# One decoder layer on one core: reloading an overwritten piece of X during the last double pair, and the low parts of two of seven pieces split on GpSimd

## The chip, the cores and the metric

The kernel runs on one core of one Trainium2 chip. The metric is the device time of one execution in microseconds (us), as a median over runs. Engines are named as in the profile: PE is TensorE (matmul), DVE is VectorE, ACT is ScalarE, POOL is GpSimd, SP is SyncE, which here issues most DMA transfers.

## The reference, cut to what matters

One step of a hybrid decoder layer in fp32, for a prompt of 1024 tokens and 8 sample tokens, model width 1024, feed-forward width 2816:

```python
x = layer_norm(ALPHA*x + 0.5*swiglu_1(x))     # first FFN
z = x @ w_in + b_in                           # projection: q k v o i f | B C h | two gates
y_a = (head_norm(mLSTM(q,k,v,i,f)) * sigmoid(o)) @ w_a
y_b = (B * conv3(C*h)) @ w_b
x = layer_norm(ALPHA*x + (sigmoid(g_a)*y_a + sigmoid(g_b)*y_b) @ w_mix)
x = layer_norm(ALPHA*x + 0.5*swiglu_2(x))     # second FFN
x = layer_norm(ALPHA*x + sigmoid(x @ w_pg) * (p @ w_pp))
```

Also returned are the mLSTM and conv states of both groups.

## The kernel before, in words

The 1032 token columns are kept in two halves of 516, and each half is worked on in blocks of 256 and 260 columns. A fp32 matrix product is made of three matmuls on numbers split into a high and a low part of type fp32r: high by high, high by low, low by high (L590, L591, L592, or L231 to L233 in other places). A split is two instructions: ACT casts the number to the high part (L274 for X, L185 for data loaded from DRAM, L416 for weights), and DVE subtracts this from the number, which gives the low part (L275, L186, L417).

Large products are not made of eight block products but of seven (Strassen-Winograd). X, hidden activations and weights therefore exist in seven pieces, which are sums and differences of blocks. The function `pair` makes such a product for one pair of weight columns. `pair2` makes a double pair, two of them at once, and applies the seven-product form once more to one inner product. For that inner product `quarters` derives smaller pieces of X, and one of these, t4, is written over a piece of X itself (`XS[1]`, in code b12). The pairs after the last double pair read that piece of X again. So it has to be reloaded from DRAM and split again, two tiles of it (kp = 0, 1): a load by SP to a tile `tmp`, the cast L274, the subtract L275. In the two FFNs this is the inner function `redo`, called at the first single pair behind the last double pair (p = 10, loop over hidden pairs p from 1; double pairs are p = 3 to 9). In the projection the same lines stand behind the loop that ends with `conv_val(3)`, and the memory-state update of the sample group follows.

Finished hidden activations go to DRAM in seven pieces (`hsum`). The output layer of an FFN takes them back in groups of hidden pairs: 3, 3 and 2 in the first FFN, 3, 3 and 3 in the second. For a group, `split_load` loads each piece (j = 0 to 6 of each pair, 128x516) and splits it (L185 on ACT, L186 on DVE). Then `segment` runs for n = 0 to 3: it makes weight pieces (sums on DVE at L425 and L428 and on POOL at L426 and L433, splits at L416 and L417) and the seven products in order j. `add` (L898, DVE) adds each finished product from PSUM onto the residual tile in SBUF, which frees the PSUM tile for a later product. PSUM tiles come from three pools, called mm, aux and pn.

```python
if j == 3:
    add(1, s, ps, OP.subtract)
elif j == 5:
    add(1, s, ps)
    add(1, s + 2, ps)
```

The list `beside` holds functions by step number; a pair calls those of its step beside its own products. `at(k, f)` puts a function there. A scheduler with priorities sets the final order of each engine's instructions; each engine then runs its own queue in that order, and waits at an instruction until what it reads is there. So an instruction that waits holds all that stands behind it in its queue.

Of the kernel before, what the change touches and what calls it, by code (L numbers as in the profile page):

```python
# [12 lines left out]
OP = mybir.AluOpType  # L13
# [3 lines left out]
NT = 1032  # L17
# [12 lines left out]
HW = 516  # L30
BN = (256, 260)
BM = 260
BLK4 = [(i // 2 * HW + i % 2 * BN[0], BN[i % 2]) for i in range(4)]
# [3 lines left out]
def F_(ap):  # L37
    return ap.bitcast(F32)
# [25 lines left out]
def layer_kernel(ctx: ExitStack, tc: tile.TileContext, I, O):  # L64
    nc = tc.nc
    V, S, G, T, DQ = nc.vector, nc.scalar, nc.gpsimd, nc.tensor, nc.sync
# [28 lines left out]
    def tmp(n=BM):  # L95
        return tmpp.tile([128, BM], F32, name="tmp", tag="tmp")[:, :n]
# [76 lines left out]
                   gen(dst[i], R) if dst else None) for i, r in enumerate(rows)]  # L173
        return [[(hi[:, j, :], lo[:, j, :]) for hi, lo in t] for j in range(4)]

    def split_load(t, src, after=nullcontext):

        hi, lo = t
        DQ.dma_start(F_(lo), src)
        with after():  # L180
            return split_here(t)

    def split_here(t):
        hi, lo = t
        S.copy(hi, F_(lo))  # L185
        V.tensor_tensor(lo, F_(lo), F_(hi), op=OP.subtract)  # L186
        return hi, lo

    ahead = {"src": {}, "live": {}, "to": {}}
# [52 lines left out]
    def bs(t, b, blk=BLK):  # L242
        c0, n = blk[b]
        return t[:, c0:c0 + n]
# [21 lines left out]
    def xparts(X7, j, kp):  # L266
        t = X7[j][kp // 2]
        return t[:, 2 * (kp % 2)], t[:, 2 * (kp % 2) + 1]
# [4 lines left out]
    def hilo(dst, src):  # L273
        order_["hi"] = S.copy(dst[0], src).ins  # L274
        order_["lo"] = V.tensor_tensor(dst[1], src, F_(dst[0]), op=OP.subtract).ins  # L275
# [26 lines left out]


    QS = ["w4", "w5", "e0"]

    def quarters(XS):

# [40 lines left out]
    def wcomb2(ra, rb):  # L348

        def k4(t):  # L350
            return t[:, 0:512].rearrange("p (k n) -> p k n", n=128)

        def put(src):
            s = slot()
            return split((k4(s), k4(s[:, 512:1024])), src)

        def fresh():
            return rawp.tile([128, 512], F32, name="raw", tag="raw")

        def blocks(r):  # L360
            return [u[:, :, i:i + 128] for u in r for i in (0, 128)]

        def sums(r):
            a11, a21, a12, a22 = blocks(r)
            s1, s2, s3 = (k4(fresh()) for _ in range(3))
            V.tensor_tensor(s1, a21, a22, op=OP.add)
            G.tensor_tensor(s3, a11, a21, op=OP.subtract)
            V.tensor_tensor(s2, s1, a11, op=OP.subtract)
            return s1, s2, s3

        def rest(r, w, s1, s2, s3):
            w[2] = put(s2)
            w[3] = put(blocks(r)[3])
            w[4] = put(s1)
            G.tensor_tensor(s2, blocks(r)[2], s2, op=OP.subtract)
            w[5] = put(s3)
            w[6] = put(s2)
            return w

        def quarter():  # L380
            half = []

            def put2(src):
                if not half:
                    s = slot()
                    half.extend([s[:, i:i + 512] for i in (0, 512)])
                t = half.pop(0)
                return split(tuple(t[:, i:i + 256].rearrange("p (k n) -> p k n", n=128) for i in (0, 256)), src)

            a11, a12, a21, a22 = (u[1][:, k:k + 2, 0:128] for u in (ra, rb) for k in (0, 2))  # L390
            s1, s2, s3, s4 = (t.rearrange("p (k n) -> p k n", n=128) for f in (fresh(), fresh())
                              for t in f.rearrange("p (a m) -> a p m", a=2))
            q = {1: put2(a12), 0: put2(a11)}
            V.tensor_tensor(s1, a21, a22, op=OP.add)
            V.tensor_tensor(s2, s1, a11, op=OP.subtract)
            G.tensor_tensor(s3, a11, a21, op=OP.subtract)
            q[4], q[2] = put2(s1), put2(s2)
            G.tensor_tensor(s4, a12, s2, op=OP.subtract)
            q[3], q[5], q[6] = put2(a22), put2(s3), put2(s4)
            return q  # L400

        t = sums(ra)
        wa = rest(ra, {0: put(blocks(ra)[0])}, *t)
        wb = {0: put(blocks(rb)[0]), 1: quarter()}
        return wa, rest(rb, wb, *sums(rb))
# [188 lines left out]
    beside = []  # L594
# [149 lines left out]
    TWO = range(3, 10)  # L744

    def ffn(wi, wo, l, XS, enter, xlate, raws, sgs, RTs, res, groups, plains, tail, extra=None, aside=None, split=None):
        hsum = tc.dram_tile([7, NHID // 2, 128, HW], F32, name=f"hsum{l}")
# [36 lines left out]
        def wi_raw(p, k):  # L784
            i = 2 * p + k
            return wraw(wi, k * FF + p * 256, raws[2 * (i % 2):2 * (i % 2) + 2])
# [45 lines left out]
                            V.scalar_tensor_tensor(d, d, 0.5, ps, op0=OP.mult, op1=OP.mult)  # L832
                        DQ.dma_start(bs(hscr[i], c, BLK4), d)

        def redo(XS):
            for kp in range(2):
                t = tmp()
                DQ.dma_start(t, bs(res[4 + kp], 1, BLK4))
                hilo(xparts(XS[1], 1, kp), t)

        enter(plain, wearly)
        sreg()
        wr = wi_raw(1, 0)
# [3 lines left out]
        for p in range(1, NHID // 2):  # L847
            if p > 1:
                sg = [gen(sgs[2 * ((p + 1) % 2) + i]) for i in range(2)]
            if p == TWO[0] - 1:  # L850
                use_ring([i for i in ring["slots"] if i not in QS])
                late = quarters(XS)
                XQ = next(late)
                at = (3, 8, 19, 24)
                beside.extend([partial(next, late)] if i in at else [] for i in range(28))
            if p == TWO[0]:
                ahead_all(aside, 7 * 24 + 28)
            if p in TWO:
                def place(i, c):
                    return bs(sg[i], c, BLK4)  # L860

                def gate(i, c, t):
                    S.activation(t, t, AF.Silu)

                def up(i, c, t):
                    d = bs(sg[i], c, BLK4)
                    V.scalar_tensor_tensor(d, d, 0.5, t, op0=OP.mult, op1=OP.mult)

                pair2(wcomb2(wi_raw(p, 0), wi_raw(p, 1)), XS, XQ, (place, lambda i, c: None), (gate, up))
            else:  # L870
                if p == TWO[-1] + 1:
                    set_ring(QS + from_ring())
                    redo(XS)
                for k in range(2):
                    hidden(k, w0 if p == 1 and k == 0 else wcomb(wi_raw(p, k)), sg, p == 1 and k == 0)
            spill(p, sg)
# [38 lines left out]
        i = 0  # L915
        for ps_, slots in groups:
            parts = {}
            for j in range(7):
                for k, p in enumerate(ps_):
                    t = gen(slots[j * len(ps_) + k], R)  # L920
                    parts[j, k] = split_load((t[:, 0:HW], t[:, HW:NT]), hsum[j, p])
            for n in range(4):
                segment(ps_, parts, n, i)
                i += 1
                order_["add", n] = order_["add"]
# [107 lines left out]
    XP = x7()  # L1033
# [301 lines left out]
    def conv_first(w, then):  # L1335
        pre_ = sg_pair()

        def out_c(i, c, fn):
            fn(bs(pre_[i], c, BLK4))

        pair(w, XP, (0, 1), out_c, True)
        for i in range(2):
            S.activation(pre_[i], pre_[i], AF.Identity, bias=bcol(CC0, i))
        then()

        def product_in(d, c0):
            def out(i, c, fn):
                t = tmp(BN[c % 2])
                fn(t)
                times(d, c0, 0)(i, c, t)  # L1350

            pair(in_pair(c0), XP, (0, 1), out)

        product_in(pre_, CH0)
        y = sg_pair()
        for i in range(2):
            conv_y(i, pre_[i], y[i])
        product_in(y, CB0)
        for i in range(2):
            DQ.dma_start(yscr[i], y[i])  # L1360

    def conv(jj):
# [4 lines left out]
        for i in range(2):  # L1367
            at(1 + 4 * i, partial(conv_y, 2 * jj + i, pre_[i], y[i]))
        return y

    def at(k, f):
        beside.extend([] for _ in range(k + 1 - len(beside)))
        beside[k].append(f)

    def conv_val(jj, y):
        d = []
        at(7, lambda: d.extend(sg_pair()))
        pair2(wcomb2(in_raw(CB0 + jj * 256), in_raw(V0 + jj * 256)), XP, XQ, (own, whole(d)),
              (times(y, CB0, jj), done), (None, lambda i: bcol(V0, 2 * jj + i)))
        for i in range(2):  # L1380
            DQ.dma_start(yscr[2 * jj + i], y[i])
        val_end(jj, d)
# [193 lines left out]
    for h in range(1, 4):  # L1576
        keys(h)
        if h < 3:
            decays(4 * h - 4)
        y = conv(h)  # L1580
        if h < 3:
            decays(4 * h - 2)
        else:
            at(6, dec_pre)
            at(14, dec_dot)
        conv_val(h, y)
    set_ring(QS + from_ring())
    for kp in range(2):
        t = tmp()
        DQ.dma_start(t, bs(x2scr[4 + kp], 1, BLK4))  # L1590
        hilo(xparts(XP[1], 1, kp), t)

    if count["sg"] % 2:
        psgs = psgs[2:] + psgs[:2]
# [529 lines left out]
    for t, nm in ((gB, "ln_g"), (bB, "ln_b")):  # L2124
        src = I[nm][0, 3]
# [9 lines left out]
    t = gen(21, R)  # L2135
# [52 lines left out]
```

## Time and profile before

| | |
|---|---|
| runs | 2645.91, 2649.43, 2652.66 us; median 2649.43 |
| the profiled execution | 2654.4 us, its span 2652.6 us |
| mean granted PE clock | 0.998 |
| busy | PE 2614.9 us (99%), DVE 2021.6 (76%), ACT 1273.0 (48%), POOL 724.8 (27%) |

A line of a list of waits reads "engine, what it was about to do <- engine, what it waited for: us in total, times, longest". A line of a timeline reads "start, duration, engine, line, operation, written tile <- read tiles, shapes", and in brackets the idle time ahead of it with what ended it; equal neighbours are drawn together (x2). A line of windows gives the stretch, its length, then busy time and count of PE, weight load, DVE, ACT and POOL, then the granted PE clock, the busy share of the DMA engines and GB/s. A line of a source line or tile gives durations in ns as min/median/max.

### The profile page before, as it was taken

The numbers are of one execution on the slowest core, as the hardware profiler recorded it, in microseconds if no ns is written. First come the engines' busy times: TensorE is split into PE (matmuls) and PEld (weight loads), VectorE is DVE, ScalarE is ACT, GpSimd is POOL, SyncE is SP. The second block draws the span as 40 slices with busy tenths as digits, with TensorE's granted clock in tenths as the row PEclk, the third lists the DMA queues.
The fourth block names the chain that finished last, engine by engine and source line by source line (L and its number), as shares of the span: only waits on it lengthen the run. The fifth ranks groups of instructions, "written<-read, shape, count | busy, mean of one in ns | idle before, by whom it ended". The sixth has DMA issues, their size and how long they took to land.

```text
span 2652.6 us, 56341 instructions
## 1 busy us (share of the span) xinstructions
PE 2614.9 (99%) x21630; PEld 2578.3 (97%) x21630; DVE 2021.6 (76%) x4356; ACT 1273.0 (48%) x2863; POOL 724.8 (27%) x724
## 2 busy tenths in 40 slices
PE   9999999999999999999999999999999999999998
PEld 9999999999999999999999999999999999999998
DVE  6877787988988777685555677748878778888787
ACT  5444446533554544445566555415445454633241
POOL 2432331112432112121110344423343233111354
PEclk9999999999999999999999999999999999999999
DMA  6244456632143343426667776832435445644421
GB/s 210 93 144 167 149 176 232 205 128 69 48 150 101 100 136 89 128 69 196 193 190 236 231 240 216 294 113 101 130 101 184 164 159 195 240 136 135 175 74 57
DMA packets 327190, 408.38 MB, mean 154 GB/s; under 512 B 30233, under 2 KB 248809, under 8 KB 326921
## 3 DMA queue, kind: packets, MB, share of 16 engines
q1 hardware_dynamic: 304600, 383.54, 44.4%
q10 hardware_dynamic: 22320, 21.26, 2.8%
q8 instruction: 169, 2.77, 0.4%
q14 instruction: 101, 0.82, 0.1%
HBM read 273.11 MB, written 131.63 MB: 153 GB/s over the span
## 4 chain that ended last, share of the span: by engine, by line
PE 87%; DVE 7%; DMA 3%; ACT 2%; issue 1%; POOL 0%; SPq 0%; DVEq 0%; ACTq 0%; POOLq 0%
PE mm L590 14%; PE mm L591 14%; PE mm L592 14%; PE mm L231 6%; PE mm L233 6%; PE mm L232 6%; PE aux L590 5%; PE aux L592 5%; PE aux L591 5%; PE pn L231 2%; PE pn L233 2%; PE pn L232 1%; PE pn L590 1%; PE pn L592 1%; PE pn L591 1%
## 5 line engine op out<-in xcount | busy, mean ns | idle before, releaser
L590 PE MATMUL mm<-a,w 128*128 128x256 f32 (+1 forms) x2289 | 646.8, 283 | 3.4 <-DVE a L898 1.7
L591 PE MATMUL mm<-a,w 128*128 128x256 f32 (+1 forms) x2289 | 644.1, 282 | 0.6 <-DVE a L275 0.5
L592 PE MATMUL mm<-a,w 128*128 128x256 f32 (+1 forms) x2289 | 643.0, 282 | 0.0
L590 PEld LDWEIGHTS mm<-a,w 128*128 128x128 f32 x2289 | 430.7, 188 | 9.3 <-issue 3.8
L591 PEld LDWEIGHTS mm<-a,w 128*128 128x128 f32 x2289 | 430.9, 188 | 1.0 <-DVE a L275 1.0
L592 PEld LDWEIGHTS mm<-a,w 128*128 128x128 f32 x2289 | 430.6, 188 | 0.5 <-issue 0.4
L590 PE MATMUL aux<-a,w 128*128 128x256 f32 (+1 forms) x852 | 241.7, 284 | 5.1 <-ACT a L274 5.0
L591 PE MATMUL aux<-a,w 128*128 128x256 f32 (+1 forms) x852 | 240.2, 283 | 0.0
L592 PE MATMUL aux<-a,w 128*128 128x256 f32 (+1 forms) x852 | 239.1, 283 | 0.0
L433 POOL TENSOR_TENSOR raw<-a,raw 128x512 f32<-128x512 f32 (+2 forms) x52 | 63.8, 1227 | 563.4 <-DVE w L417 203.6
L231 PE MATMUL mm<-a,w 128*128 128x256 f32 (+4 forms) x727 | 208.0, 288 | 2.0 <-ACT w L1683 1.8
L232 PE MATMUL mm<-a,w 128*128 128x256 f32 (+4 forms) x727 | 207.1, 286 | 0.0
L590 PE MATMUL mm<-a,e 128*128 128x256 f32 (+1 forms) x694 | 196.7, 283 | 2.6 <-DVE a L898 1.5
L591 PE MATMUL mm<-a,e 128*128 128x256 f32 (+1 forms) x694 | 195.4, 282 | 0.0
L592 PE MATMUL mm<-a,e 128*128 128x256 f32 (+1 forms) x694 | 195.3, 281 | 0.0
L233 PE MATMUL mm<-a,w 128*128 128x256 f32 (+4 forms) x681 | 192.7, 286 | 0.0
L590 PEld LDWEIGHTS aux<-a,w 128*128 128x128 f32 x852 | 161.3, 189 | 7.6 <-ACT a L274 5.4
L591 PEld LDWEIGHTS aux<-a,w 128*128 128x128 f32 x852 | 161.4, 190 | 0.0
L592 PEld LDWEIGHTS aux<-a,w 128*128 128x128 f32 x852 | 160.7, 190 | 0.4 <-issue 0.4
L590 PE MATMUL mm<-a,cd 128*128 128x260 f32 (+1 forms) x520 | 147.4, 284 | 1.4 <-ACT sreg L623 0.6
L591 PE MATMUL mm<-a,cd 128*128 128x260 f32 (+1 forms) x520 | 146.8, 282 | 0.0
L344 ACT CAST w<-raw 128x512 fp32r<-128x512 f32 (+1 forms) x179 | 96.5, 549 | 104.7 <-PE aux L592 40.1
(629 smaller groups left out, 8274.0 us busy)
## 6 DMA issues: line engine op xcount, KB each, us to landing
a<-in_ffn_wi_dram SPq DMA_DIRECT2D x80, 512.0 KB
a<-in_w_in_dram SPq DMA_DIRECT2D x68, 512.0 KB
a<-hsum SPq DMA_DIRECT2D x119, 258.0 KB
wscr<-w SPq DMA_DIRECT2D x35, 512.0 KB
hsum<-a SPq DMA_DIRECT2D x68, 258.0 KB
a<-in_ffn_wo_dram SPq DMA_DIRECT2D x40, 384.0 KB
w<-wscr SPq DMA_DIRECT2D x25, 512.0 KB
a<-in_state_C_dram ACTq DMA_DIRECT2D x32, 256.0 KB
```

Source lines behind the costliest of these rows:

```text
L231: T.matmul(ps, wh, xh, start=(i == 0), stop=False)
L232: T.matmul(ps, wh, xl, start=False, stop=False)
L233: last = T.matmul(ps, wl, xh, start=False, stop=(i == n - 1))
L344: S.copy(dst[0], src)
L433: G.tensor_tensor(s4, a12, s2, op=OP.subtract)
L590: T.matmul(ps, wh, xh, start=start and kp == 0, stop=False, skip_group_check=True)
L591: T.matmul(ps, wh, xl, start=False, stop=False, skip_group_check=True)
L592: T.matmul(ps, wl, xh, start=False, stop=stop and kp == len(xs) - 1, skip_group_check=True)
```

## The change: earlier reloads, and 34 subtracts on POOL

There are three edits. First, `redo` no longer runs behind the last double pair: it puts the two loads at steps 16 and 17 and the two splits at steps 18 and 20 of that double pair's `beside` list. This holds for both FFNs and for the projection. Second, for pieces j = 5 and 6 (products six and seven) of the output layers, the subtract L186 runs on POOL. These are 34 instructions: 6, 6 and 4 in the first FFN's groups, 6, 6 and 6 in the second's. Third, in `conv_first` the second `conv_y` runs beside step 1 of the following product.

```diff
-    def split_load(t, src, after=nullcontext):
+    def split_load(t, src, after=nullcontext, eng=None):
         hi, lo = t
         DQ.dma_start(F_(lo), src)
         with after():
-            return split_here(t)
+            return split_here(t, eng)
 
-    def split_here(t):
+    def split_here(t, eng=None):
         hi, lo = t
         S.copy(hi, F_(lo))
-        V.tensor_tensor(lo, F_(lo), F_(hi), op=OP.subtract)
+        (eng or V).tensor_tensor(lo, F_(lo), F_(hi), op=OP.subtract)
...
+    def redo(XS, src):
+        t = {}
+        def load(kp):
+            t[kp] = tmp()
+            DQ.dma_start(t[kp], bs(src[4 + kp], 1, BLK4))
+        def split_(kp):
+            hilo(xparts(XS[1], 1, kp), t.pop(kp))
+        for kp in range(2):
+            at(16 + kp, partial(load, kp))
+            at(18 + 2 * kp, partial(split_, kp))
...
-        def redo(XS):
-            for kp in range(2):
-                t = tmp()
-                DQ.dma_start(t, bs(res[4 + kp], 1, BLK4))
-                hilo(xparts(XS[1], 1, kp), t)
...
+                if p == TWO[-1]:
+                    redo(XS, res)
                 pair2(wcomb2(wi_raw(p, 0), wi_raw(p, 1)), XS, XQ, (place, lambda i, c: None), (gate, up))
             else:
                 if p == TWO[-1] + 1:
                     set_ring(QS + from_ring())
-                    redo(XS)
...
-                    parts[j, k] = split_load((t[:, 0:HW], t[:, HW:NT]), hsum[j, p])
+                    parts[j, k] = split_load((t[:, 0:HW], t[:, HW:NT]), hsum[j, p], eng=G if j > 4 else V)
...
-        for i in range(2):
-            conv_y(i, pre_[i], y[i])
+        conv_y(0, pre_[0], y[0])
+        at(1, partial(conv_y, 1, pre_[1], y[1]))
         product_in(y, CB0)
...
             at(6, dec_pre)
             at(14, dec_dot)
+            redo(XP, x2scr)
         conv_val(h, y)
     set_ring(QS + from_ring())
-    for kp in range(2):
-        t = tmp()
-        DQ.dma_start(t, bs(x2scr[4 + kp], 1, BLK4))
-        hilo(xparts(XP[1], 1, kp), t)
```

In the changed kernel the lines behind these edits have other numbers: L416/L417 are L435/L436, L425, L428 and L433 are L444, L447 and L452, L426 is L445, L898 is L912, L627/L628 are L646/L647, L1402, L1516 and L1524 are L1412, L1526 and L1534. L185, L186, L274 and L275 keep theirs.

What moves on ACT in the projection. Before, the two casts L274 to a_9287 (the piece of X) stand behind L1524, the first use of a loaded memory state, and an activation-table load:

```order
L1516 DMA a_16245<-in_state_C_dram 128x2x256 x2
L1524 ACTIVATE a_16244<-a_16244,zer,wkb 128x512
L416 CAST w_16542<-raw 128x512
L1402 ACT_TABLE_LOAD
L1402 ACTIVATE a_16242<-a_16242,pc 128x256
L416 CAST w_16793<-a_16786 128x512
L274 CAST a_9287<-tmp 128x260 x2
```

After, on the same engine:

```order
L690 ACTIVATE a_15858<-mm,pc 128x256
L363 CAST e_15699<-raw 128x512
L435 CAST w_16261<-a_16251 128x512
L274 CAST a_9287<-tmp 128x260 x2
L690 ACTIVATE a_15858<-mm,pc 128x260
L435 CAST w_16271<-raw 128x512
```

They now stand among the double pair's own evictions and weight casts, 31 rows ahead of L1534 (the new number of L1524).

What moves on DVE in the first FFN's output layer, second group. a_7051 to a_7071 are pieces six and seven of the group's three hidden pairs, a_6151 to a_6172 residual tiles. Before:

```order
L417 TENSOR_TENSOR e_7265<-a_7258,e_7265 128x384
L898 TENSOR_TENSOR a_6151<-a_6151,mm 128x256
L186 TENSOR_TENSOR a_7051<-a_7051 128x516
L186 TENSOR_TENSOR a_7055<-a_7055 128x516
L898 TENSOR_TENSOR a_6172<-a_6172,pn 128x260
L186 TENSOR_TENSOR a_7059<-a_7059 128x516
L428 TENSOR_TENSOR raw<-raw,a_7258 128x384
L898 TENSOR_TENSOR a_6169<-a_6169,mm 128x256
L186 TENSOR_TENSOR a_7063<-a_7063 128x516
L417 TENSOR_TENSOR w_7277<-a_7260,w_7277 128x384
```

After, on DVE, and in a second block on POOL:

```order
L436 TENSOR_TENSOR e_7265<-a_7258,e_7265 128x384
L912 TENSOR_TENSOR a_6151<-a_6151,mm 128x256
L912 TENSOR_TENSOR a_6172<-a_6172,pn 128x260
L447 TENSOR_TENSOR raw<-raw,a_7258 128x384
L912 TENSOR_TENSOR a_6169<-a_6169,mm 128x256
L436 TENSOR_TENSOR w_7277<-a_7260,w_7277 128x384
```

```order
L445 TENSOR_TENSOR raw<-a_7258 128x384
L186 TENSOR_TENSOR a_7051<-a_7051 128x516
L186 TENSOR_TENSOR a_7055<-a_7055 128x516
L186 TENSOR_TENSOR a_7059<-a_7059 128x516
L186 TENSOR_TENSOR a_7063<-a_7063 128x516
L186 TENSOR_TENSOR a_7067<-a_7067 128x516
L186 TENSOR_TENSOR a_7071<-a_7071 128x516
L452 TENSOR_TENSOR raw<-a_7260,raw 128x384
```

The adds keep their order; the six subtracts stand on POOL between two sums of weights.

What stands on DVE around the reload in the second FFN (a_24233 is the piece of X, a_30348 and a_30352 are hidden pieces). Before:

```order
L417 TENSOR_TENSOR e_30068<-raw,e_30068 128x512
L275 TENSOR_TENSOR a_24233<-tmp,a_24233 128x260 x2
L417 TENSOR_TENSOR w_30073<-raw,w_30073 128x512
L425 TENSOR_TENSOR raw<-a_30400,a_30402 128x384
L632 TENSOR_TENSOR a_29793<-sreg,mm 128x256
L186 TENSOR_TENSOR a_30348<-a_30348 128x516
L186 TENSOR_TENSOR a_30352<-a_30352 128x516
```

After, at the place where the single pair's first evictions stand:

```order
L436 TENSOR_TENSOR e_30062<-raw,e_30062 128x512
L436 TENSOR_TENSOR cd<-a_30048,cd 128x512
L186 TENSOR_TENSOR a_30352<-a_30352 128x516
L186 TENSOR_TENSOR a_30348<-a_30348 128x516
L646 SCALAR_TENSOR_TENSOR a_29802<-sreg,mm 128x256
L647 TENSOR_TENSOR a_29802<-sreg,mm 128x256
```

L275 now stands 41 rows ahead of these; the two L186 come before evictions of the pair that follows.

More of the change, by code (lines that the diff above doesn't have):

```diff
@@ L304, in layer_kernel, with at @@
     QS = ["w4", "w5", "e0"]
+    def at(k, f):
+        beside.extend([] for _ in range(k + 1 - len(beside)))
+        beside[k].append(f)
+    def redo(XS, src):
[8 more added lines that the diff above has]
+            at(18 + 2 * kp, partial(split_, kp))
     def quarters(XS):
@@ L1369, in conv @@
         return y
-    def at(k, f):
-        beside.extend([] for _ in range(k + 1 - len(beside)))
-        beside[k].append(f)
     def conv_val(jj, y):
```

## The prediction

> **What bounds the kernel now.** I read the busy times, then what TensorE (PE) waited for, then the queues behind the longest waits, and last the places where the moved operations stand.
>
> ```profile
> span 2652.6 us, 56341 instructions
> PE 2614.9 (99%) x21630; PEld 2578.3 (97%) x21630; DVE 2021.6 (76%) x4356; ACT 1273.0 (48%) x2863; POOL 724.8 (27%) x724
> ...
> PE aux L590 <- ACT a L274: 5.0, 2, 2.6
> PE mm L590 <- DVE a L898: 3.2, 7, 0.8
> PE pn L590 <- DVE a L898: 1.4, 3, 0.8
> PE aux L592 <- DVE e L417: 1.2, 1, 1.2
> ```
>
> PE is idle for 2652.6 - 2614.9 = 37.7 us in all, so an edit that takes no matmul away can win only from these idle times and from the clock. The list of waits (total, times, longest) names the two that the change aims at: 5.0 us for the ACT cast of the reloaded piece (two waits), and 3.2 + 1.4 = 4.6 us for L898, the DVE add of a finished product onto the residual, which frees a PSUM tile (ten waits). The list has no third wait on the reload: of the three reloads, that of the first FFN is hidden already, and the order of its instructions on ACT and SP stays, so I count it at 0.
>
> The two waits on the reload, in the timeline of PE, and the granted clock (the number ahead of the DMA share) in the stretches behind them and behind the 1.2 us wait on L417:
>
> ```profile
> 1219.46 0.51 PE L590 MATMUL aux<-a,w 128*128 128x260 f32 x2 [2.41 <-ACT a L274]
> 2252.65 0.39 PE L590 MATMUL aux<-a,w 128*128 128x260 f32 x1 [2.58 <-ACT a L274]
> ...
> 603.00:606.00 3.00, 3.00 (x26) 3.00 (x27) 3.00 (x10) 0.93 (x3) 0.74 (x1) 1.00 0.00 0
> 1219.40:1225.00 5.60, 5.54 (x33) 5.54 (x34) 3.21 (x8) 2.73 (x8) 0.00 (x0) 0.70 0.23 70
> 2252.60:2259.00 6.40, 6.35 (x40) 6.35 (x41) 4.88 (x10) 3.83 (x9) 1.25 (x1) 0.73 0.69 220
> ```
>
> After both idle times of 2.4 us or more the clock stood at 0.70 and 0.73 for some 6 us; after the one of 1.2 us it stayed at 1.00. That is a second loss: 5.60 x 0.30 = 1.7 us and 6.40 x 0.27 = 1.7 us. So the two reloads cost 5.0 + 3.4 = 8.4 us, more than the list of waits shows.
>
> **The reload, moved into the last double pair.** Per place: two DMA loads on SP, two casts L274 on ACT, two subtracts L275 on DVE; none is added or removed, all stand earlier. What held them before:
>
> ```profile
> ACT a L1524 <- DMA a<-in_state_C_dram: 4.9, 1, 4.9
> ...
> 1215.45 0.81 ACT L1524 ACTIVATE a<-a,zer,wkb 128x512 f32<-128x512 f32 x1 [4.92 <-DMA a<-in_state_C_dram]
> 1219.00 0.72 ACT L274 CAST a<-tmp 128x260 fp32r<-128x260 f32 x2
> ...
> 2248.44 0.99 SPq L838 DMA_DIRECT2D tmp<-rscr  x2
> 2252.19 0.76 ACT L274 CAST a<-tmp 128x260 fp32r<-128x260 f32 x2 [4.92 <-DMA tmp<-rscr]
> ```
>
> In the projection ACT stood at L1524, waiting 4.9 us for a state load, with the casts in its queue behind that. In the second FFN the loads were only issued at 2248.44, and ACT waited for them to 2252.19. In the new order the casts stand 30 or so rows of ACT earlier, and the loads some 20 rows of SP earlier, amid double-pair work that has products to run. The moved steps take 2 x 0.36 us of ACT and 0.8 us of DVE from engines at 48% and 76%, and the two loads (0.99 us of SP) stand ahead of weight loads that are taken up many us later: 0, covered by the double pair; if that cover were gone it would be at most these 0.7 to 1.0 us.
>
> What is late next: in the projection L1524 itself. It still waits for the state to 1215.45, and a product of the state update that needs what follows it comes earlier on PE in the new order: between 0 and 2 us of new idle, I take 1. In the second FFN two casts and two L186 of hidden sums, whose loads are issued behind a weight store after that pair's last spill, now stand ahead of L646/L647 (by the old lines L627/L628), which free PSUM: between 0 and 2 us, I take 0.5. An idle time under 1.3 us leaves the clock alone, so both clock losses go. Sum: -8.4 + 1.5 = -6.9 us; ends -8.4 and, if both next waits are 2 us or more and take the clock with them, 0.
>
> **The second conv_y beside the next pair.** The DVE order changes only behind 803 us, and from there to 1219 the list of PE's waits is empty: 0, covered by the running pair; uncovered it is one piece of DVE work of a few us at most, and PE has products to run beside it.
>
> **The subtracts on POOL.** 6 + 6 + 4 in the first FFN's three groups and 6 + 6 + 6 in the second's, 34 in all. In the first FFN's second group:
>
> ```profile
> 520.40 0.63 ACT L185 CAST a<-a 128x516 fp32r<-128x516 f32 x1
> 526.23 0.62 ACT L185 CAST a<-a 128x516 fp32r<-128x516 f32 x1 [1.01 <-DMA a<-hsum]
> ...
> 526.00:533.00 7.00, 5.58 (x42) 4.82 (x41) 7.00 (x16) 3.23 (x6) 0.00 (x0) 1.00 0.46 132
> 521.04 0.54 DVE L425 TENSOR_TENSOR raw<-a,a 128x384 f32<-128x384 f32 x1
> 525.73 0.54 DVE L417 TENSOR_TENSOR e<-a,e 128x384 fp32r<-128x384 f32 x1
> 526.20 0.41 DVE L898 TENSOR_TENSOR a<-a,mm 128x256 f32<-128x256 f32 x1
> 526.53 1.29 DVE L186 TENSOR_TENSOR a<-a 128x516 fp32r<-128x516 f32 x2
> 531.17 0.41 DVE L898 TENSOR_TENSOR a<-a,mm 128x260 f32<-128x260 f32 x1
> ...
> 526.66 0.38 PE L590 MATMUL mm<-a,w 128*128 128x256 f32 x1 [0.30 <-DVE a L898]
> 526.88 0.28 PE L591 MATMUL mm<-a,w 128*128 128x256 f32 x1
> 527.00 0.28 PE L592 MATMUL mm<-a,w 128*128 128x256 f32 x1
> 531.72 0.36 PE L590 MATMUL mm<-a,e 128*128 128x256 f32 x1 [0.78 <-DVE a L898]
> ```
>
> The two casts are the first and the last of the six concerned; DVE is busy for all of the 7.00 us in the row of the window (third busy time). Six of its L186 from 526.53 on are the ones that leave, 1.29 / 2 = 0.65 us each, and PE's waits from 526.66 to 531.72 end with the L898 between them. Such waits lie in this group and in the second and third of the second FFN, as the lists of PE's waits from 500 to 560 and from 2280 to 2420 show:
>
> ```profile
> PE mm L590 <- DVE a L898: 1.1, 2, 0.8
> PE pn L590 <- DVE a L898: 0.3, 1, 0.3
> ...
> PE mm L590 <- DVE a L898: 1.7, 4, 0.8
> PE pn L590 <- DVE a L898: 0.8, 1, 0.8
> ```
>
> That is 3.9 of the 4.6 us. Were POOL free of charge, they would largely go, with the slow first matmuls behind each: the lower end, -5. But the casts of the six end between 521.03 and 526.85, so POOL would run them while DVE does earlier work. What both cost at the same time:
>
> ```profile
> L186 DVE TENSOR_TENSOR a<-a x119: 679/685/1462, 430.0 to 2414.4; 128x516 fp32r<-128x516 f32 x119
> L898 DVE TENSOR_TENSOR a<-a,mm x230: 404/411/427, 463.6 to 2464.8; 128x256 f32<-128x256 f32 x68, 128x260 f32<-128x260 f32 x47
> L1708 POOL TENSOR_TENSOR a<-a,a x28: 1188/1203/1748, 1472.5 to 1660.4; 128x516 fp32r<-128x516 f32 x28
> ...
> 519.54 1.02 POOL L426 TENSOR_TENSOR raw<-a 128x384 f32<-128x384 f32 x1 [2.65 <-DVE w L417]
> 519.72 1.40 DVE L186 TENSOR_TENSOR a<-a 128x516 fp32r<-128x516 f32 x1
> ...
> 823.26 1.13 POOL L330 TENSOR_TENSOR tmp<-a 128x260 f32<-128x260 f32 x1 [0.36 <-DVE a L1328]
> 824.34 1.48 POOL L367 TENSOR_TENSOR raw<-a 128x512 f32<-128x512 f32 x1
> 823.70 3.28 DVE L1328 SCALAR_TENSOR_TENSOR a<-tmp,pc,a 128x260 f32<-128x260 f32 x3
> ```
>
> The same L186 is 0.685 us at the median and 1.40 when a POOL operation of 1.02 us began 0.18 us ahead of it: it ran behind that operation (520.56 + 0.6 = 521.1). At 823.70 three DVE operations take 1.09 us each with POOL busy: the two engines take turns. L898, which reads PSUM, keeps to 0.404-0.427 whatever POOL does.
>
> By strict turns: a subtract of this shape is 1.20 us on POOL (L1708, same shape). From 521.04 to 526.20 DVE has seven operations on SBUF alone (L425 to L417, 5.16 us with four L898 of 0.33 between, so 3.84 without). Six POOL operations in between make it 521.0 + 7.2 + 3.84 = 532.1 for the L898 that now starts at 526.20, 5.9 later. After it DVE has less to do, and PE's later waits go: three products of nine matmuls at 0.12 are 3.2 us, the time from 526.66 to 531.72 is 5.06, so 1.8 were waits. +5.9 - 1.8 = +4.1 for this group. The second FFN's second group has the same spacing (+4); its third has the subtracts a little later against the adds, and I put it at +3; the other three have more slack, +1 together. Upper end +12. I take +8: the only rows in which both engines have work show turns (1.40, 1.09), but POOL will not always stand at its next instruction when DVE lets go, and some turns fall where DVE waits for a product.
>
> The Trainium skill has the turns as a rule: "SBUF — State Buffer", SBUF: two separate sides, says that a VectorE operation with two SBUF inputs and a GpSimd operation take a shared port pair as an exclusive lock for the whole instruction. "Perfetto Trace Analysis", Optimizing Scalar/DVE Operations, adds that moving work between the two might therefore not help. The rows agree (1.40 against 0.685, and no change for L898). By that rule without exception POOL's part would be the upper end, +12; by the view that the engines work side by side, -5.
>
> Sum: -6.9 + 0 + 8 = +1.1. The profiled execution took 2654.4 us (its span 2652.6 and 1.8 around it), 5.0 above the median of the runs, 2649.43; I put the same difference on the median: 2650.5.
>
> **Rivals.**
> POOL's subtracts are free: they fall beside DVE's work, and the adds come in time. For it: POOL is at 27% and was idle for 2.65 us ahead of 519.54. Against: 1.40 us at 519.72. -6.9 - 5 = -12, 2637.5.
> The reload gains nothing: the product waits just as long for the state load, or for the hidden sums. For it: the 4.9 us of L1524 stay. Against: nothing of what that product reads stands behind L1524 any more. 0 + 8 = +8, 2657.5.
> Strict turns throughout: for it the rows at 823; against, POOL is idle for microseconds around each of its operations here. -6.9 + 12 = +5, 2654.5.
> Slower, by the clock: the late L898 of an output group make one idle time of PE instead of several short ones. If it passes a length between 1.2 and 2.4 us, the clock goes to 0.7 for 6 us as behind the reload, 1.7 us for each of three groups: -6.9 + 12 + 5 = +10, 2659.5. It decides as soon as two add-to-product waits fall together; against it, products of 1.3 us each start as tiles come free one by one.
>
> **Chances.** Forecast 0.40, strict turns 0.17, POOL free 0.20, reload without gain 0.09, clock in the output groups 0.14. A change under 0.3% (7.9 us) can hardly be told from none; the three runs shown lie 6.8 us apart. Faster means below 2641.5: nearly all of the POOL-free case, 0.18, and 0.04 of the forecast's spread: 0.22. Slower means above 2657.4: most of the clock case, half of the reload case and a little of the strict turns: 0.18. Same: 0.60. The range reaches to just above the free case and to the clock case, 2638 to 2660, and leaves out the outer half of each: under 0.2.
>
> **What would show it.** Right: no idle above 1.3 us and a clock of 1.00 where the reloads' products start; L186 on POOL at 1.2 us or more; L186, L417 and L425 on DVE beside it at 1.1 to 1.9 us, L898 unchanged; PE's waits on L898 in three output groups larger than 4.6 us in all. Wrong: POOL's 34 operations with DVE at 0.68 beside them; a wait of 2 us or more at the first product behind the last double pair; the clock below 1.00 in an output group.

## The result and the profile after

The changed kernel takes 2673.42 us at the median, against 2650.84 before: the ratio is 1.0083, with a 95% interval of 1.0071 to 1.0094, so +22.0 us (+18.8 to +24.9); the medians themselves lie 22.6 us apart. That is slower, and outside the range of the prediction. The page of the changed kernel, and its list of PE's waits:

```profile
span 2671.7 us, 56360 instructions
PE 2622.4 (98%) x21630; PEld 2584.6 (97%) x21630; DVE 2031.8 (76%) x4322; ACT 1272.1 (48%) x2863; POOL 777.0 (29%) x758
...
PE mm L609 <- DVE a L912: 14.5, 11, 2.7
PE mm L609 <- ACT sreg L642: 2.7, 2, 2.2
...
PE aux L611 <- DVE w L436: 1.8, 1, 1.8
PE pn L609 <- DVE a L912: 1.8, 2, 1.1
PE aux L609 <- DVE a L631: 1.7, 1, 1.7
...
PE aux L609 <- DVE a L912: 1.3, 1, 1.3
```

The 5.0 us for the cast of the reloaded piece are gone. The waits on the add (L898 before, L912 now) are 14.5 + 1.8 + 1.3 = 17.6 us in place of 4.6, +13.0. New are 2.2 us on an eviction by ACT (L642), 1.8 us on a weight split (L436) and 1.7 us on a DVE add (L631). DVE has 34 operations fewer and yet 10 us more of busy time. The same instructions, in the view of the lines L186 and L912:

```profile
L186 DVE TENSOR_TENSOR a<-a x85: 680/693/1785, 428.3 to 2424.9; 128x516 fp32r<-128x516 f32 x85
L186 POOL TENSOR_TENSOR a<-a x34: 1283/1608/1761, 464.2 to 2425.4; 128x516 fp32r<-128x516 f32 x34
...
L912 DVE TENSOR_TENSOR a<-a,mm x230: 403/413/427, 460.9 to 2484.7; 128x256 f32<-128x256 f32 x77, 128x260 f32<-128x260 f32 x38
```

A subtract on POOL takes 1.61 us at the median, where this shape takes 1.20 alone. The second output group of the first FFN, in the timelines of POOL, DVE and PE:

```profile
520.51 8.37 POOL L186 TENSOR_TENSOR a<-a 128x516 fp32r<-128x516 f32 x5
...
521.36 1.45 DVE L186 TENSOR_TENSOR a<-a 128x516 fp32r<-128x516 f32 x1
522.73 1.64 DVE L436 TENSOR_TENSOR cd<-raw,cd 128x384 fp32r<-128x384 f32 x1
524.29 0.41 DVE L912 TENSOR_TENSOR a<-a,mm 128x256 f32<-128x256 f32 x1
524.62 1.43 DVE L186 TENSOR_TENSOR a<-a 128x516 fp32r<-128x516 f32 x1
527.67 1.62 DVE L436 TENSOR_TENSOR e<-a,e 128x384 fp32r<-128x384 f32 x1
529.22 0.41 DVE L912 TENSOR_TENSOR a<-a,mm 128x256 f32<-128x256 f32 x1
...
526.44 0.39 PE L609 MATMUL mm<-a,w 128*128 128x260 f32 x1 [2.66 <-DVE a L912]
529.68 0.58 PE L609 MATMUL mm<-a,w 128*128 128x256 f32 x1 [1.73 <-DVE a L912]
```

Five subtracts fill POOL without a gap, 1.67 us each. The DVE operations on SBUF shown beside them take 1.43 to 1.64 us, where in the kernel before they took 0.54 to 0.68 with POOL idle; the adds from PSUM keep their 0.41, but stand behind the others in DVE's queue. So they come late, and PE is idle twice, for 2.66 and 1.73 us. Nothing waits for the subtracts on POOL themselves: in the view of L186 on POOL, the list of who waited for it is empty. The clock behind such idle times, in windows:

```profile
529.60:534.60 5.00, 4.92 (x24) 4.92 (x25) 5.00 (x14) 1.56 (x3) 0.00 (x0) 0.53 0.25 79
2288.00:2292.50 4.50, 3.99 (x20) 3.99 (x21) 4.50 (x6) 2.19 (x4) 3.16 (x3) 0.62 1.06 403
2357.00:2364.00 7.00, 5.81 (x26) 5.51 (x27) 7.00 (x15) 1.56 (x3) 2.71 (x2) 0.51 0.19 53
2424.50:2432.50 8.00, 6.40 (x31) 6.10 (x32) 8.00 (x17) 1.47 (x2) 2.67 (x2) 0.57 0.19 51
```

In four output groups it stood at 0.51 to 0.62. The 101 matmuls of these windows took 21.1 us of PE's busy time; at the 0.12 us of before they take 12.1. That is about 9 us more, the restarts included. The two profiled executions differ by 19.1 us in span (2671.7 against 2652.6): PE's busy time grew by 7.5 us and its idle time by 11.6. In the busy time, the 9 us and one more stretch of low clock, behind the wait on L642, stand against the two behind the reloads that went. In the idle time, the 13.0 us on the add and the 5.7 us of the other new waits stand against the 5.0 us of the reload and smaller waits that went.

### The profile page after: what moved, and what is told of

Same layout as the page of the kernel before. It is cut to its first block, busy times and chain, and to the rows that moved or that the text cites. A ratio compares the mean times of both kernels' runs of the same rounds, so it can differ in the third digit from the quotient of the medians.

```text
span 2671.7 us, 56360 instructions
## 1 busy us (share of the span) xinstructions
PE 2622.4 (98%) x21630; PEld 2584.6 (97%) x21630; DVE 2031.8 (76%) x4322; ACT 1272.1 (48%) x2863; POOL 777.0 (29%) x758
## 4 chain that ended last, share of the span: by engine, by line
PE 83%; DVE 9%; DMA 3%; issue 2%; ACT 2%; POOL 1%; SPq 0%; DVEq 0%; ACTq 0%; POOLq 0%
PE mm L609 14%; PE mm L611 13%; PE mm L610 13%; PE mm L231 6%; PE mm L232 6%; PE mm L233 6%; PE aux L609 5%; PE aux L610 5%; PE aux L611 5%; PE pn L231 2%; PE pn L233 1%; PE pn L232 1%; DVE a L186 1%; DVE w L436 1%; DMA a<-hsum 1%
## 5 line engine op out<-in xcount | busy, mean ns | idle before, releaser
L609 PE MATMUL aux<-a,w 128*128 128x260 f32 (+1 forms) x852 | 241.2, 284 | 1.3 <-DVE a L912 1.3
L611 PE MATMUL aux<-a,w 128*128 128x256 f32 (+1 forms) x852 | 239.1, 283 | 1.8 <-DVE w L436 1.8
L610 PE MATMUL aux<-a,w 128*128 128x260 f32 (+1 forms) x852 | 240.0, 282 | 0.0
L452 POOL TENSOR_TENSOR raw<-a,raw 128x512 f32<-128x512 f32 (+2 forms) x52 | 63.1, 1214 | 509.9 <-issue 191.2
L609 PE MATMUL mm<-a,e 128*128 128x260 f32 (+1 forms) x694 | 197.9, 285 | 3.3 <-DVE a L912 2.2
L610 PE MATMUL mm<-a,e 128*128 128x260 f32 (+1 forms) x694 | 196.2, 283 | 0.0
L611 PE MATMUL mm<-a,e 128*128 128x260 f32 (+1 forms) x694 | 196.0, 282 | 0.0
```

The costliest lines, as they stand in the source:

```text
L609: T.matmul(ps, wh, xh, start=start and kp == 0, stop=False, skip_group_check=True)
L610: T.matmul(ps, wh, xl, start=False, stop=False, skip_group_check=True)
L611: T.matmul(ps, wl, xh, start=False, stop=stop and kp == len(xs) - 1, skip_group_check=True)
```

## The experiments

All were timed beside the kernel before on the same chip, whose median there was 2650.85 to 2651.03 us. Differences are the ratio less one, times that.

**The three parts apart.** First, all but the subtracts:

```diff
-parts[j, k] = split_load(..., hsum[j, p], eng=G if j > 4 else V)
+parts[j, k] = split_load(..., hsum[j, p])
```

> The changed kernel with the 34 subtracts back on DVE; reloads and conv_y stay early. Theory A (POOL and DVE take strict turns, and the idle time this gives PE lowers the clock, so nearly all of the +22.6 us is the POOL part): -4 to 0 us against before, with no PE wait above 1 us on L912 in the output layers. Theory B (the reloads' new order delays the casts and splits of the output layers, and POOL adds only the +8 predicted): +10 to +15 us.

Measured: ratio 1.0005 (0.9996 to 1.0013), +1.3 us (-1.1 to +3.4). That is a little above theory A's range, with an interval that reaches into it, and far below theory B's. The waits on the add are back at what they were, 3.4 + 1.2 = 4.6 us, the longest 0.8:

```profile
PE mm L609 <- ACT sreg L642: 4.1, 3, 2.0
PE mm L609 <- DVE a L912: 3.4, 8, 0.8
PE pn L609 <- DVE a L912: 1.2, 3, 0.8
```

The subtracts alone, put into the kernel before:

```diff
-parts[j, k] = split_load(..., hsum[j, p])
+parts[j, k] = split_load(..., hsum[j, p], eng=G if j > 4 else V)
```

> Before with only the 34 subtracts on POOL. Theory A: +18 to +24 us, L186 on POOL near 1.7 us beside DVE operations of 1.4 to 1.6 us, PE clock below 0.8 for some us in at least three output groups. Theory B: +5 to +10 us.

Measured: 1.0092 (1.0080 to 1.0104), +24.4 us (+21.2 to +27.6). With the run before, theory B falls: the 34 subtracts are the whole loss. Their trace has 12.8 + 4.7 = 17.5 us of waits on the add, against 4.6:

```profile
PE mm L590 <- DVE a L898: 12.8, 10, 2.7
PE pn L590 <- DVE a L898: 4.7, 3, 3.9
...
1222.41 0.50 PE L590 MATMUL aux<-a,w 128*128 128x260 f32 x2 [0.62 <-ACT a L274]
```

The last line is the projection's reload, here in its old place: 0.62 us of idle where the profiled execution of before had 2.41. The wait that the change aims at there differs from one profiled execution to the next.

The projection's reload alone, by the new `redo` in its `conv_val(3)`, the FFNs' as before:

> Before with only the projection's reload early. Theory A: -4.2 us (2.6 us of idle and 1.6 us of low clock gone, nothing late next). Theory B: 0, since L1524 still waits 4.9 us for the state and something behind it is late next. A stall of 1.8 us near 833 us that the changed kernel has should be absent if it comes from conv_y.

Measured: 0.9993 (0.9984 to 1.0001), -1.9 us (-4.2 to +0.3). Smaller than the -4.2 of theory A, and the interval reaches it and 0; the varying wait can account for the difference from -4.2, since six of the seven profiled executions with the reload in its old place show shorter waits than 2.41 us and no low clock behind them (numbers in the next section). The stall near 833 us is absent.

The second `conv_y` alone:

> Before with only the second conv_y beside the next product. By the prediction 0. By the trace after, a stall of PE of 1.8 us near 833 us (PE waits for the DVE operation L612, behind DVE and POOL work of the conv): +2 us.

Measured: 1.0008 (0.9999 to 1.0016), +2.1 us (-0.3 to +4.2). The timelines of PE and DVE in this kernel, and then DVE in the kernel before, show where it comes from:

```profile
829.33 0.39 PE L590 MATMUL aux<-a,e 128*128 128x260 f32 x1 [1.67 <-DVE a L612]
...
824.51 3.30 DVE L1328 SCALAR_TENSOR_TENSOR a<-tmp,pc,a 128x260 f32<-128x260 f32 x3
827.73 1.21 DVE L366 TENSOR_TENSOR raw<-a,a 128x512 f32<-128x512 f32 x1
828.87 0.41 DVE L612 TENSOR_TENSOR a<-sreg,aux 128x256 f32<-128x256 f32 x1
...
826.91 0.41 DVE L612 TENSOR_TENSOR a<-sreg,aux 128x256 f32<-128x256 f32 x1
827.24 0.90 DVE L366 TENSOR_TENSOR raw<-a,a 128x512 f32<-128x512 f32 x1
```

This stall stands in all three kernels that have the edit (the changed one, the first run and this one), and in none of the nine others. DVE now runs the weight sum L366, 1.21 us, ahead of the L612 that ends it; in the kernel before it stood behind that. That the edit costs is likely, that it costs 2 us is not settled by the interval.

**Why the subtracts cost.** The rival was that they are late on POOL, so that what reads them waits. So DVE kept its subtracts, and POOL got work that nobody reads, at the same places in its queue:

```diff
 S.copy(hi, F_(lo))
+if eng is G:
+    G.tensor_tensor(tmp(), F_(hi)[:, 0:BM], F_(hi)[:, HW - BM:HW], op=OP.subtract)
 V.tensor_tensor(lo, F_(lo), F_(hi), op=OP.subtract)
```

> Before, DVE keeps all its subtracts, and POOL makes at the 34 places a subtract of 128x260 of the piece's high part into a scratch tile that nothing reads. Theory A (turns at a shared port): +10 to +22 us, since each such operation holds up a DVE operation by 0.7 to 1.0 us and DVE is relieved of nothing; DVE's L186-like subtracts at 1.2 to 1.5 us beside it. Rival C (the changed kernel is slow because the low parts come later from POOL, so products or DVE operations wait for them): 0 to +3 us, since nothing reads the result.

Measured: 1.0042 (1.0028 to 1.0055), +11.1 us (+7.4 to +14.6). Work whose result nothing reads costs 11 us, so lateness of POOL's results is not needed for a loss. It does not have to explain the rest either, and rival C falls: no instruction waited for POOL's L186 in the changed kernel, and with the subtracts alone ACT did once, for 0.8 us. The cost here is about half of +24.4 because PE's waits on the add are 9.0 + 1.9 + 0.9 = 11.8 us in place of 17.5, and the clock stays at 1.00 in every output group. In the timelines (this kernel's subtract on DVE is L188, its weight split L419):

```profile
521.14 1.23 DVE L188 TENSOR_TENSOR a<-a 128x516 fp32r<-128x516 f32 x1
523.44 1.10 DVE L419 TENSOR_TENSOR cd<-raw,cd 128x384 fp32r<-128x384 f32 x1
...
520.05 2.92 POOL L187 TENSOR_TENSOR tmp<-a 128x260 f32<-128x260 f32 x3 [0.40 <-ACT a L185]
```

DVE's operations are longer beside POOL's here too, but by less; POOL's operation is half as wide and takes 0.97 us in place of 1.67.

The same with a copy, one input in place of two:

```diff
-    G.tensor_tensor(tmp(), F_(hi)[:, 0:BM], F_(hi)[:, HW - BM:HW], op=OP.subtract)
+    G.tensor_copy(tmp(), F_(hi)[:, 0:BM])
```

> As the run before, with a copy of 128x260 (one input) on POOL in place of the subtract (two inputs). Theory A, if any POOL operation on SBUF takes the turn: +6 to +18 us, in proportion to the shorter operation. If only two-input operations of POOL hold DVE up: 0 to +3 us. Rival C: 0 to +3 us.

Measured: 1.0006 (0.9997 to 1.0015), +1.6 us (-0.8 to +4.0), less than theory A expected of any operation on SBUF. By the timeline the copy does hold DVE up, but for some 0.2 us. It is also shorter than the subtract (median 0.73 against 1.06 us), so this run does not separate the one input from the shorter time:

```profile
521.05 0.89 DVE L188 TENSOR_TENSOR a<-a 128x516 fp32r<-128x516 f32 x1
522.80 0.75 DVE L419 TENSOR_TENSOR cd<-raw,cd 128x384 fp32r<-128x384 f32 x1
...
520.86 1.34 POOL L187 COPY tmp<-a 128x260 f32<-128x260 f32 x2 [0.76 <-ACT a L185]
```

Half the dose, product seven alone (17 in place of 34):

```diff
-eng=G if j > 4 else V
+eng=G if j > 5 else V
```

> Before with the subtract on POOL for product seven alone (17 in place of 34). Theory A with the clock loss: less than half of the +24 us, +5 to +10 us, since three turns make PE idle for under 2 us and the clock stays at 1.00. Were the cost even per operation: +12 us.

Measured: 1.0041 (1.0027 to 1.0054), +10.9 us (+7.2 to +14.3). The interval holds both expectations, so this does not tell them apart. What the trace does show is that the expected reason was wrong: the clock did not stay at 1.00. It fell behind idle times of 2.16, 1.91 and 1.92 us in three output groups; the first and the last in windows:

```profile
527.40:531.00 3.60, 3.51 (x18) 3.54 (x19) 3.60 (x10) 0.52 (x1) 0.00 (x0) 0.56 0.34 96
2411.00:2415.00 4.00, 3.80 (x19) 3.80 (x20) 4.00 (x10) 1.20 (x2) 0.00 (x0) 0.57 0.01 3
...
2411.20 0.50 PE L590 MATMUL mm<-a,e 128*128 128x256 f32 x1 [1.92 <-DVE a L898]
```

The subtracts on POOL only in the first FFN's first and third groups (10 of the 34):

```diff
-eng=G if j > 4 else V
+eng=G if j > 4 and l == 0 and i in (0, 8) else V
```

> Before with the subtract on POOL only in the first and third output group of the first FFN (6 + 4 = 10 of the 34), where the adds have slack. If it is the place that counts (PE waits only where the delayed adds have no slack): +1 to +3 us. Were the cost even per operation (24.4 us over 34): +7 us.

Measured: 1.0006 (0.9997 to 1.0015), +1.6 us (-0.8 to +4.0). That is below the +7 of an even cost. It is the place that counts: in these two groups the waits on the add grow from 0.7 to 1.8 us only and no low clock follows, while the four others are those in which the changed kernel shows the low clock.

**The reloads.** All three early, nothing else changed:

> All three reloads early, nothing else changed. If the wait of L642 behind the casts took the place of the second FFN's reload, and only the reordering of those casts brought the gain of the version with them moved: -2 us against before, the projection's part alone. If the gain came from leaving conv_y where it was: -4 us, as with the casts moved.

Measured: 0.9993 (0.9984 to 1.0002), -1.9 us (-4.2 to +0.5). In the second FFN the timelines of ACT and PE of this kernel show what is late next, and the window the clock behind it:

```profile
2249.22 0.62 ACT L185 CAST a<-a 128x516 fp32r<-128x516 f32 x1 [5.28 <-DMA a<-hsum]
2250.21 0.62 ACT L185 CAST a<-a 128x516 fp32r<-128x516 f32 x1 [0.37 <-DMA a<-hsum]
2250.74 0.37 ACT L642 COPY sreg<-mm 128x260 f32<-128x260 f32 x1
...
2251.16 0.39 PE L609 MATMUL mm<-a,w 128*128 128x260 f32 x1 [1.93 <-ACT sreg L642]
...
2251.00:2255.50 4.50, 4.34 (x23) 4.34 (x24) 4.50 (x9) 3.03 (x8) 1.91 (x2) 0.62 0.31 123
```

ACT waits 5.28 us for a load at a cast, the eviction L642 stands behind it, and PE waits for that PSUM tile. So the last run orders these two casts behind the first single pair's last eviction, and leaves the loads where they are:

```diff
+if k == 0:
+    order_["snap0"] = order_["snap"]      # the pair's last eviction
 ...
+after = partial(tc.issue_after, order_["snap0"]) if l and i == 0 and j * len(ps_) + k in (8, 9) else nullcontext
-parts[j, k] = split_load(..., hsum[j, p])
+parts[j, k] = split_load(..., hsum[j, p], after)
```

> Only the reloads early (conv_y and the subtracts as before), and in the second FFN the two casts L185 that stood ahead of the evictions L642 issued behind them. Theory (what took the reload's place there was the wait of L642 behind casts that wait 5.7 us for their loads): -5 to -8 us against before. Rival (the loads of the hidden pieces come too late in any order, and the next wait takes the gain again): -1 to -4 us.

Measured: 0.9986 (0.9977 to 0.9994), -3.7 us (-6.1 to -1.6). ACT now evicts first and waits afterwards, and PE's wait there is 0.6 us:

```profile
2249.11 0.38 ACT L642 COPY sreg<-mm 128x260 f32<-128x260 f32 x1 [1.06 <-PE mm L611]
2254.37 1.15 ACT L185 CAST a<-a 128x516 fp32r<-128x516 f32 x2 [3.85 <-DMA a<-hsum]
...
PE mm L609 <- ACT sreg L642: 0.6, 1, 0.6
```

This version, reloads early and two casts behind the eviction, is faster than both kernels. Its gain lies between the two expectations: less than the -5 of the theory, and within the -1 to -4 of the rival. Its interval overlaps that of the run without the order, so how much the order alone is worth is not settled by the times; PE's wait, 0.6 us in place of 1.93, shows what it does.

## Why the prediction was wrong

**The subtracts, taken at +8, measured +24.4.** The mechanism was right: turns, and the adds late behind DVE's other work, though no slower themselves. The sizes of two terms were wrong, the waiting (+8) and the low clock, which was left out of the sum.
- The term of waiting was put between -5 and +12, and +8 was taken because POOL "will not always stand at its next instruction when DVE lets go". It does stand there: 8.37 us for five operations without a gap. The waits on the add grew by 13.0 us (17.6 against 4.6), a little over the upper end. In the three groups worked out by strict turns (+4.1, +4, +3) they grew by 3.0, 3.2 and 3.2; in the other three, put at +1 together, by 3.5. The page of the Trainium skill that was weighed there, "SBUF — State Buffer", SBUF: two separate sides, had the exclusive lock, by which the prediction came to +12. The rows above agree with it nearly: a turn of both engines took 1.67 us, where the durations without the other, 1.20 and 0.54 to 0.69, add up to 1.74 to 1.89.
- The clock behind the new idle times was a rival with a chance of 0.14 and +5 us. It came in four groups, about 9 us, and was one of the prediction's own signs of being wrong. In three of the four the clock stayed low for 6.8 us, since PE was idle again for 1.1 to 1.7 us at the low clock. The argument against it, that tiles come free one by one, failed: the adds came bunched, 529.22 and then four more within 2.3 us, and PE was idle for 2.66 and 1.73 us.
- The second FFN's first group was among "the other three, +1 together". PE waited there 1.8 us for the weight split L436, which also takes turns with POOL, and at a clock of 0.62 behind it. Only the L898 had been looked at as what PE waits for.

**The reloads, taken at -6.9, measured -1.9 (-4.2 to +0.5).** The steps moved as described, at no cost of their own. Two terms failed.
- The 8.4 us were those of one profiled execution. In the seven profiled kernels that leave the projection's reload in its old place, PE is idle there for 0.22 to 2.41 us, 1.4 on average, and only in the longest, the kernel before, does a low clock follow. In the eight that leave the second FFN's reload, it is 1.93 to 2.73 us, 2.25 on average, with a low clock behind five. With 1.7 us for each low clock, that makes an estimate of 1.4 + 2.25 + 0.2 + 1.1, about 5 us to be won on average.
- "What is late next" in the second FFN was named rightly, the casts of the hidden pieces ahead of PSUM evictions, but taken at 0.5 us of a range of 0 to 2, and read on DVE (L646). It was 1.9 to 2.2 us in three profiled kernels, on ACT's L642, and in two of them it took the clock with it (0.62 in the row above). Of the 5 us a wait of 1.9 us and 1.7 us of low clock leave 1.4, and -1.9 was measured; with the casts ordered away a wait of 0.6 us is left, so 4.4, and -3.7 was measured.
- In the projection the wait taken at 1 us did not come: in the list after no wait stands behind L1534, the old L1524.

**conv_y, taken at 0, measured +2.1 (-0.3 to +4.2),** with a stall of 1.67 us on L612. The prediction's ground for 0, that the list of PE's waits is empty there, says nothing of how much slack there is.

The sum of the parts, 24.4 - 1.9 + 2.1 = 24.6, agrees with the +22.0 (+18.8 to +24.9) measured for the whole.

## What to carry to other kernels

Work moved from DVE to POOL is not taken off DVE where both work on SBUF: find a row in which the two overlap, take its longer duration as the price for every neighbour in DVE's queue, and then look at who waits for operations that stand behind those neighbours, weights and evictions too. When a wait is removed by moving a load earlier, read the queue of every engine behind it for an instruction that waits for a DMA and has an eviction behind it, since that one can take its place; here only the version with two casts ordered behind the eviction was measurably faster than the kernel before. And take a wait that hangs on a DMA's arrival as one that varies (here 0.22 to 2.41 us), not as a sum to be won in full.

## What the runs showed of the hardware that was not expected

How long PE is idle does not alone decide whether the clock falls; it also matters when. Behind 1.93 us of idle in the run with all reloads early (2249.23 to 2251.16) it fell; behind 1.95 us in the run with subtracts in two groups (2248.12 to 2250.07) it stayed at 1.00. Windows of 3.4 us show the difference, first in the former run and then in the latter:

```profile
2248.38:2251.78 3.40, 1.47 (x13) 1.27 (x12) 1.61 (x3) 2.19 (x5) 0.00 (x0) 1.00 0.53 152
2251.79:2255.19 3.40, 3.40 (x18) 3.40 (x18) 3.40 (x7) 2.24 (x6) 1.60 (x2) 0.50 0.38 154
...
2250.07 0.38 PE L590 MATMUL aux<-a,w 128*128 128x260 f32 x1 [1.95 <-ACT a L274]
...
2245.06:2248.46 3.40, 3.07 (x26) 2.87 (x25) 2.24 (x3) 0.26 (x1) 2.12 (x2) 1.00 0.89 271
2248.47:2251.87 3.40, 1.80 (x15) 1.80 (x16) 1.75 (x4) 1.24 (x3) 0.45 (x2) 1.00 0.92 309
2251.88:2255.28 3.40, 3.40 (x30) 3.40 (x30) 1.93 (x4) 1.57 (x3) 1.04 (x1) 1.00 0.76 279
```

Apart from their first 16 us and last 9 us, the granted clock in the twelve traces is 1.00 or 0.50 and nothing else, and it changes only at times that lie a whole number of stretches of 3.413 us apart. In the changed kernel it is low from 527.47 to 534.30, 2261.44 to 2264.86, 2288.75 to 2292.16, 2357.02 to 2363.84 and 2425.28 to 2432.11: the first two falls are 1733.97 us apart, 508 stretches. After a stretch at full clock, PE's idle time in that stretch goes with what follows: with 1.77 us or more (20 cases) the next was at 0.50, with 1.61 us or less at 1.00, and between 1.62 and 1.68 us one of four fell. That is about half of a stretch. The 1.93 us lie in one stretch; the 1.95 us are cut by the border at 2248.46 into 0.34 and 1.61.

So the prediction's length "between 1.2 and 2.4 us" is no threshold for a single idle time. Its clocks of 0.70 and 0.73 over some 6 us are one stretch of 3.41 us at 0.50 each, averaged with full clock; the loss of 1.7 us is the same. In the Trainium skill, "TensorE: Matmul & The Clock Gate", Part 1, the clock follows activity windows of about 3.4 us that run free of the program. The stretches here agree with that length. The page has the clock low after a whole idle window; here half of one was enough, and the measurement decides.
